# VectorE's order by tile, fixed between the stages of a two-layer encoder

## The chip, the cores and the metric

The kernel runs on one core of one Trainium2 chip. The metric is the device time of one execution in microseconds (us). Before the change three runs took 866.87, 868.81 and 868.93 us, with a median of 868.81 us.

## The reference

The program is an encoder of two layers over 16 learned tokens and 256 input tokens (272 in all) with 1024 channels. In each layer a token mixer and an MLP stand one after the other, and each is wrapped in two norms:

```python
for l in range(DEPTH):                                   # 2 layers
    u = rms_norm(h, norm_mix_pre[l])
    proj = u @ w_in[l]                                   # q, k, v, gates
    y_r = retention_branch(...) @ w_ret_o[l]
    y_a = attention_branch(...) @ w_att_o[l]
    mix = (sigmoid(gate_r) * y_r + sigmoid(gate_a) * y_a) @ w_mix_o[l]
    h = h + rms_norm(mix, norm_mix_post[l])
    u = rms_norm(h, norm_ff_pre[l])
    ff = square(relu(u @ w_ff1[l])) @ w_ff2[l]
    h = h + rms_norm(ff, norm_ff_post[l])
return h[:, N_META:]
```

`rms_norm(x, g)` is `x * rsqrt(mean(x * x) + 1e-6) * g`. `h` is the residual stream. The change touches the two lines that update `h` and the `rms_norm` that reads it at once afterwards.

## The kernel before

**Layout.** Channels lie on the partitions and tokens on the free axis. `h` is eight tiles of 128 channels by 272 tokens (`h[:, k]`, k from 0 to 7). In the second layer's MLP only the last 256 tokens are kept.

**Weights.** 260 units of 128x1024 floats come in turn from memory. `unit` (from L120) reads a unit into `raw`, ScalarE rounds it to `wh` (L131), and VectorE takes the remainder `wl = raw - wh` (L132). The activations are split in the same way. A product of a weight block and an activation tile is three matmuls (L136 to L138): high by high, high weight by low activation (`ul`), low weight by high activation (`uh`). A unit holds eight blocks, one for each `k`, so it is 24 matmuls into one PSUM accumulator. There are four buffers for `wh` and `wl` and three for `raw`.

**Between the stages.** `leave` (L293) drains the products of a stage, scales them into `yg[:, m]` and sums their squares. A mean over the channels is a TensorE product with a constant matrix (L183). Ten matmuls on zeros (L178, `warm(10)`) follow it on TensorE. `rsqrt` makes the factor `y` with Ln and Exp on ScalarE. `leave` hands back `update(k)`. For tile 0 this is four operations of VectorE (L315 and three at L93): `yg` times `y`, a Newton step on it, `h[0]` plus the result, and `y1`, the factor that the other seven tiles use. For each later tile it is two: `yg[k] = -0.5 * yg[k] * y1` and `h[k] = h[k] + yg[k]` (L321).

`enter` (L225) runs `update(k)` for each tile and splits the new `h[k]` times a gain into `uh` (ScalarE, L242) and `ul` (VectorE, through the helper `stt`, so L93). Where the norm asks for it, it also squares `h[k]` (ScalarE, L222) and adds the squares (VectorE, L234, L236). The next stage's products take one tile of `uh` and `ul` at a time. Its first four units are under way at the same time in four accumulators, so a tile feeds twelve matmuls.

**Where this happens.** Three places in the program have a `leave` that is followed by an `enter` with an `update`: the middle of layer 0 (mix to MLP, from 251 us), the border of the layers (MLP of layer 0 to the projections of layer 1, from 447 us) and the middle of layer 1 (from 681 us). They are called the first, second and third place below. The MLP of layer 1 ends in another code.

**What sets the order.** Each engine works through its own list in order. A scheduler makes these lists from the recorded operations when the program is built, by priorities and its own estimates of time. `tc.issue_after(x)` tells it that an operation comes after `x` in its list. At the three places nothing of this kind stands on the operations of `update` and `enter`, so that the scheduler alone decides.

Of the kernel before, what the change touches and what calls it, by code (L numbers as in the profile page):

```python
# [19 lines left out]
KD = D // P  # L20
# [21 lines left out]
def encoder(ctx: ExitStack, tc: tile.TileContext, order, w, h_in, gains, dec, decm, sink, sinkm, tabs, mats, esel, masks, rel, relm, grow, out):  # L42
    nc = tc.nc
    V, A, PE, G = nc.vector, nc.scalar, nc.tensor, nc.gpsimd
    mul, add, sub, mn = ALU.mult, ALU.add, ALU.subtract, ALU.min
# [15 lines left out]
    def slot(i, name, shape=(KD, T), dt=F32):  # L61
        return big.tile([P] + list(shape), dt, tag=f"b{i}", name=name)
# [7 lines left out]
    def tokens(i, name, shape=(KD,), at=32):  # L70
        return slot(i, name, (*shape, ROW), F32R)[..., at:at + T]
# [17 lines left out]
    def f(t):  # L89
        return t.bitcast(F32)  # L90

    def stt(o, a, s, b, op0=mul, op1=mul):
        V.scalar_tensor_tensor(out=o, in0=a, scalar=s, in1=b, op0=op0, op1=op1)  # L93

    def split(xh, xl, x):
        A.activation(xh, x, AF.Copy)  # L96
# [78 lines left out]
    def warm(n):  # L175
        ps = bank("t", [P])
        for _ in range(n):
            tc.keep_in_program_order(PE.matmul(ps, idle, idle, start=True, stop=True))  # L178

    def mean(parts, c0):  # L180
        ms = bank("o", [T])
        for i, p in enumerate(parts):
            PE.matmul(ms[:, c0:], mat["o1024"], p[:, c0:], start=i == 0, stop=i == len(parts) - 1)  # L183
        return ms

    def rsqrt(y1, ms, c0):
        y = two.tile([P, T], F32, tag="t1", name="y")
        w2 = two.tile([P, T], F32, tag="t2", name="w2")
        A.activation(y[:, c0:], ms[:, c0:], AF.Ln)
        A.activation(y[:, c0:], y[:, c0:], AF.Exp, scale=-0.5)  # L190
        return y, w2, newton(None if y1 is None else y1[:, c0:], ms[:, c0:], 0.0, y[:, c0:], w2[:, c0:])

    warm(WARM)
    h = const.tile([P, KD, T], F32, name="h")
    g = const.tile([P, DEPTH, 4, KD], F32, name="g")
# [24 lines left out]
    def square(src, c0):  # L220
        sq = two.tile([P, T], F32, tag="sq", name="sq", bufs=3)
        A.activation(sq[:, c0:], src, AF.Square)  # L222
        return sq

    def enter(l, n, c0, update):  # L225
        x = [tokens(i, "u" + "hl"[i], at=32 - 16 * l) for i in range(2)]
        ss = one.tile([P, T], F32, tag="ss", name="ss")

        lag = KD if n else LAG0

        def accumulate(k):
            sq = square(h[:, k, c0:], c0)
            if k == 0:
                V.tensor_scalar(out=ss[:, c0:], in0=sq[:, c0:], scalar1=8e-6, scalar2=None, op0=add)  # L234
            else:
                V.tensor_tensor(out=ss[:, c0:], in0=ss[:, c0:], in1=sq[:, c0:], op=add)  # L236

        for k in range(KD):
            if update:
                update(k)  # L240
            gk = g[:, l, n, k:k + 1]
            A.activation(x[0][:, k, c0:], h[:, k, c0:], AF.Copy, scale=gk)  # L242
            stt(x[1][:, k, c0:], h[:, k, c0:], gk, f(x[0][:, k, c0:]), op1=sub)
            if k >= lag:
                accumulate(k - lag)
        if update and n == 0:
            for k in range(KD - lag, KD):
                accumulate(k)
        return x, ss, accumulate
# [46 lines left out]
    def leave(l, n, c0, products, init=None):  # L296
        yg = slot(4, "yg")
        ss = one.tile([P, T], F32, tag="ss", name="ss2")
        for m, ps in products:
            sq = square(ps[:, c0:], c0)  # L300
            A.activation(yg[:, m, c0:], ps[:, c0:], AF.Copy, scale=g[:, l, n, m:m + 1])
            if m == 0 and init is None:
                V.tensor_scalar(out=ss[:, c0:], in0=sq[:, c0:], scalar1=8e-6, scalar2=None, op0=add)
            elif m < KD - 1:
                V.tensor_tensor(out=ss[:, c0:], in0=(init if m == 0 else ss)[:, c0:], in1=sq[:, c0:], op=add)
        y1 = one.tile([P, T], F32, tag="rb", name="y1")
        ms = mean([ss, sq], c0)
        warm(10)
        y, w2, sq = rsqrt(None, ms, c0)
        held[len(order) + 3] = [sq.ins]  # L310

        def update(k):
            yk = yg[:, k, c0:]
            if k == 0:
                V.tensor_tensor(out=yk, in0=yk, in1=y[:, c0:], op=mul)  # L315
                stt(yk, w2[:, c0:], 3.0, yk, op0=sub)
                stt(h[:, k, c0:], yk, -0.5, h[:, k, c0:], op1=add)
                stt(y1[:, c0:], w2[:, c0:], 3.0, y[:, c0:], op0=sub)
            else:
                stt(yk, yk, -0.5, y1[:, c0:])  # L320
                V.tensor_tensor(out=h[:, k, c0:], in0=h[:, k, c0:], in1=yk, op=add)  # L321

        return update

# [11 lines left out]
    lows, odds = slice(64, 128), (slice(32, 64), slice(96, 128))  # L336
# [26 lines left out]
    for l in range(DEPTH):  # L363
        c0 = 16 * l
        if l == 0:
            u, ss, early = lead()
        else:
            u, ss, _ = enter(l, 0, 0, update)
            early = [proj(u, 0, "asas"[i], "v_r", i) for i in range(4)]
# [193 lines left out]
        if l == 0:  # L563
# [6 lines left out]
            for c in range(4):  # L570
                V.tensor_tensor(
                    out=pmblk.rearrange("p (t c g k) -> p t c g k", t=4, c=4, g=2)[:, :, c],
                    in0=mat["blk"].rearrange("p (t g k) -> p t g k", t=4, g=2),
                    in1=pm[:, 0:16].unsqueeze(1).unsqueeze(1).to_broadcast([P, 4, 2, 16]),
                    op=mul,
# [187 lines left out]
        def mixed():  # L763
            pair = [product(z, c0, wide(), "mix", m) for m in range(2)]
            for p in pair:
                for _ in range(KD - 1):
                    next(p)
            for m in range(KD):
                *_, (_, ps) = pair[m] if m < 2 else product(z, c0, wide(), "mix", m)
                yield m, ps  # L770

        update = leave(l, 1, c0, mixed())

        u, ss, accumulate = enter(l, 2, c0, update)
        fs, behind = [], []

# [7 lines left out]
        for m in range(KF):  # L784
            if m % KD == 0:
                a, b = ((5, 7), (8, 9), (6, 10), (2, 3))[m // KD]
                low = [tokens(i, "fl", (4,), 32 - c0) for i in ("10a", "10b")] if b == 10 else [tokens(b, "fl", at=32 - c0)]
# [13 lines left out]
        if l == 0:  # L801
            def ff2():
                for m in range(KD):
                    ps = bank(wide(), [T])
                    for q in range(4):
                        wh, wl = unit("ff2", m, q)
                        for k in range(KD):
                            sl = slice(k * P, (k + 1) * P)
                            mm3(ps[:, c0:], wh[:, sl], wl[:, sl], fs[q][0][k][:, c0:], fs[q][1][k][:, c0:], q == 0 and k == 0, q == 3 and k == KD - 1)
                    yield m, ps  # L810

            update = leave(l, 3, c0, ff2(), e2)
# [180 lines left out]
```

## Time and profile before

| | |
|---|---|
| median of three runs | 868.81 us (866.87 to 868.93) |
| the profiled execution | 874.68 us, with a span of 872.9 us |
| TensorE matmuls, busy | 854.7 us (98% of the span) |
| VectorE busy | 608.5 us (70%) |
| ScalarE busy | 564.8 us (65%) |
| mean granted TensorE clock | 0.996 of full |

The span runs from the first to the last instruction of the profiled execution. That execution is 5.87 us longer than the median of the runs without a profile. Busy time of TensorE is that of instructions which overlap, so that 98% does not mean 98% of its peak. The stretches in which TensorE has no matmul are found in the timeline, where a row has in brackets the idle time before it and what ended it.

### The profile page before, as it was taken

How to read it: one execution, taken by the hardware profiler on the slowest of the kernel's cores; microseconds unless marked ns; L12 is line 12 of the kernel's file. 1: busy time of each engine (PE TensorE's matmuls, PEld its weight loads, DVE VectorE, ACT ScalarE, POOL GpSimd, SP SyncE). 2: the span in 40 equal slices, each digit the busy share in tenths (PEclk: the TensorE clock that was granted, in tenths of full speed). 3: DMA queues.
4: the chain of work that ended last, by engine and by line, in shares of the span. 5: the costliest groups of instructions: out<-in, count | busy, mean ns of one | idle time of the engine just before them, and what ended most of it. 6: DMA issues, size and time to landing. Idle time of an engine off the chain costs nothing.

```text
span 872.9 us, 16696 instructions
## 1 busy us (share of the span) xinstructions
PE 854.7 (98%) x6514; PEld 822.2 (94%) x6514; DVE 608.5 (70%) x1129; ACT 564.8 (65%) x1050; POOL 50.6 (6%) x114
## 2 busy tenths in 40 slices
PE   9999999999999999999999999999999999999997
PEld 8899999999989999999989999999999999998885
DVE  7889888878668555444468898888786775554544
ACT  7448788675558777544455578987845587783432
POOL 2112220000000000000000122200000000000000
PEclk9999999999999999999999999999999999999999
DMA  8544443446545655655635544434376276666661
GB/s 293 194 125 139 122 130 114 145 146 192 164 128 179 190 179 178 176 184 172 178 112 153 162 132 141 141 124 148 115 219 200 90 239 189 183 193 194 190 192 70
DMA packets 41407, 142.15 MB, mean 163 GB/s; under 512 B 5360, under 2 KB 6256, under 8 KB 41328
## 3 DMA queue, kind: packets, MB, share of 16 engines
q1 hardware_dynamic: 40896, 140.43, 52.3%
q8 instruction: 51, 0.84, 0.4%
q10 hardware_dynamic: 432, 0.66, 0.2%
q14 instruction: 28, 0.23, 0.1%
HBM read 140.02 MB, written 1.05 MB: 162 GB/s over the span
## 4 chain that ended last, share of the span: by engine, by line
PE 80%; DVE 10%; ACT 6%; issue 1%; DMA 1%; POOL 0%; SPq 0%; DVEq 0%; ACTq 0%; POOLq 0%
PE ps_a L136 12%; PE ps_a L137 12%; PE ps_a L138 12%; PE ps_s L138 5%; PE ps_s L136 5%; PE ps_s L137 5%; PE ps_t L136 4%; PE ps_t L137 4%; PE ps_t L138 4%; DVE wl L132 3%; PE ps_s L853 2%; PE ps_a L853 2%; PE ps_a L855 2%; PE ps_s L855 2%; PE ps_s L854 2%; PE ps_a L854 2%
## 5 line engine op out<-in xcount | busy, mean ns | idle before, releaser
L132 DVE TENSOR_TENSOR wl<-raw,wh 128x1024 fp32r<-128x1024 f32 x256 | 313.0, 1224 | 199.7 <-ACT wh L131 198.2
L131 ACT ACTIVATE wh<-raw 128x1024 fp32r<-128x1024 f32 x256 | 269.8, 1058 | 204.4 <-PE ps_a L137 62.3
L136 PE MATMUL ps_a<-uh,wh 128*128 128x272 f32 (+1 forms) x912 | 263.0, 289 | 2.8 <-ACT uh L242 2.8
L138 PE MATMUL ps_a<-uh,wl 128*128 128x272 f32 (+1 forms) x912 | 260.0, 285 | 0.5 <-DVE wl L132 0.3
L137 PE MATMUL ps_a<-ul,wh 128*128 128x272 f32 (+1 forms) x912 | 260.1, 286 | 0.0
L136 PEld LDWEIGHTS ps_a<-uh,wh 128*128 128x128 f32 x912 | 172.6, 189 | 3.8 <-ACT uh L242 3.2
L138 PEld LDWEIGHTS ps_a<-uh,wl 128*128 128x128 f32 x912 | 172.9, 190 | 1.2 <-DVE wl L132 0.8
L137 PEld LDWEIGHTS ps_a<-ul,wh 128*128 128x128 f32 x912 | 172.4, 189 | 0.4
L138 PE MATMUL ps_s<-uh,wl 128*128 128x272 f32 (+1 forms) x184 | 52.4, 285 | 0.3 <-DVE wl L132 0.3
L137 PE MATMUL ps_s<-ul,wh 128*128 128x272 f32 (+1 forms) x184 | 52.3, 284 | 0.0
L136 PE MATMUL ps_s<-uh,wh 128*128 128x272 f32 (+1 forms) x184 | 52.2, 284 | 0.0
L136 PE MATMUL ps_t<-uh,wh 128*128 128x272 f32 (+1 forms) x152 | 43.5, 286 | 1.3 <-ACT uh L242 1.3
L137 PE MATMUL ps_t<-ul,wh 128*128 128x272 f32 (+1 forms) x152 | 43.5, 286 | 0.0
L138 PE MATMUL ps_t<-uh,wl 128*128 128x272 f32 (+1 forms) x152 | 43.2, 284 | 0.0
L138 PEld LDWEIGHTS ps_s<-uh,wl 128*128 128x128 f32 x184 | 34.9, 190 | 0.5 <-DVE wl L132 0.5
L136 PEld LDWEIGHTS ps_s<-uh,wh 128*128 128x128 f32 x184 | 34.7, 189 | 0.0
L137 PEld LDWEIGHTS ps_s<-ul,wh 128*128 128x128 f32 x184 | 34.6, 188 | 0.0
L136 PEld LDWEIGHTS ps_t<-uh,wh 128*128 128x128 f32 x152 | 28.6, 188 | 1.5 <-ACT uh L242 1.5
L138 PEld LDWEIGHTS ps_t<-uh,wl 128*128 128x128 f32 x152 | 28.9, 190 | 0.0
L137 PEld LDWEIGHTS ps_t<-ul,wh 128*128 128x128 f32 x152 | 28.6, 188 | 0.1
L97 DVE TENSOR_TENSOR fl<-ft,fh 128x272 fp32r<-128x272 f32 (+1 forms) x64 | 27.6, 433 | 1.0 <-ACT fh L96 0.9
L96 ACT ACTIVATE fh<-ft 128x272 fp32r<-128x272 f32 (+1 forms) x64 | 27.2, 425 | 1.7
(311 smaller groups left out, 1963.5 us busy)
## 6 DMA issues: line engine op xcount, KB each, us to landing
raw<-in_w SPq DMA_DIRECT2D x256, 512.0 KB, 3.7
leads<-in_w SPq DMA_DIRECT2D x6, 256.0 KB, 5.6
tab<-in_tabs SPq DMA_DIRECT2D x2, 544.0 KB, 6.3
h<-in_h_in SPq DMA_DIRECT2D x3, 272.0 KB, 5.8
out<-yt SPq DMA_DIRECT2D x3, 256.0 KB, 2.1
leads<-in_w ACTq DMA_DIRECT2D x2, 256.0 KB, 3.4
gj<-in_grow SPq DMA_DIRECT2D x1, 512.0 KB, 4.7
mats<-in_mats SPq DMA_DIRECT2D x1, 320.0 KB, 7.2
```

What stands on the lines that cost most here:

```text
L96: A.activation(xh, x, AF.Copy)
L97: V.tensor_tensor(out=xl, in0=x, in1=f(xh), op=sub)
L131: A.activation(wh[:, c], raw[:, c], AF.Copy)
L132: V.tensor_tensor(out=wl[:, c], in0=raw[:, c], in1=f(wh[:, c]), op=sub)
L136: PE.matmul(ps, ah, bh, start=first, stop=False)
L137: PE.matmul(ps, ah, bl, start=False, stop=False)
L138: return PE.matmul(ps, al, bh, start=False, stop=last)
L853: PE.matmul(pss[i], xh, wh[:, sl], start=kk == 0, stop=False)
L854: PE.matmul(pss[i], xh, wl[:, sl], start=False, stop=False)
L855: PE.matmul(pss[i], xl, wh[:, sl], start=False, stop=kk == KF - 1)
```

## The change

At the three places the operations of VectorE are put in a chain, each told to come after the one before. The chain begins with `h[0]`, then `y1`, and then for each next tile `yg[k]`, `h[k]`, and the low part `ul` of the tile before. The sums of squares, where there are any in this loop, are in the chain too. The first two operations of `update(0)` and the splits of weights (`wl`) are not in it.

```diff
     def stt(o, a, s, b, op0=mul, op1=mul):
-        V.scalar_tensor_tensor(out=o, in0=a, scalar=s, in1=b, op0=op0, op1=op1)
+        return V.scalar_tensor_tensor(out=o, in0=a, scalar=s, in1=b, op0=op0, op1=op1)
...
         lag = KD if n else LAG0
+        line, lows = [], []
+
+        def next_in_line(method, *args, **kw):
+            with ExitStack() as later:
+                if line and update:
+                    later.enter_context(tc.issue_after(line[-1]))
+                line.append(method(*args, **kw).ins)
...
         for k in range(KD):
+            gk = g[:, l, n, k:k + 1]
             if update:
-                update(k)
-            gk = g[:, l, n, k:k + 1]
+                update(k, next_in_line)
             A.activation(x[0][:, k, c0:], h[:, k, c0:], AF.Copy, scale=gk)
-            stt(x[1][:, k, c0:], h[:, k, c0:], gk, f(x[0][:, k, c0:]), op1=sub)
+            low = (x[1][:, k, c0:], h[:, k, c0:], gk, f(x[0][:, k, c0:]))
+            if update:
+                lows.append(low)
+                for low in lows[:-1] if k < KD - 1 else lows:
+                    next_in_line(stt, *low, op1=sub)
+                del lows[:-1]
+            else:
+                stt(*low, op1=sub)
...
-        def update(k):
+        def update(k, put):
             yk = yg[:, k, c0:]
             if k == 0:
                 V.tensor_tensor(out=yk, in0=yk, in1=y[:, c0:], op=mul)
                 stt(yk, w2[:, c0:], 3.0, yk, op0=sub)
-                stt(h[:, k, c0:], yk, -0.5, h[:, k, c0:], op1=add)
-                stt(y1[:, c0:], w2[:, c0:], 3.0, y[:, c0:], op0=sub)
+                put(stt, h[:, k, c0:], yk, -0.5, h[:, k, c0:], op1=add)
+                put(stt, y1[:, c0:], w2[:, c0:], 3.0, y[:, c0:], op0=sub)
             else:
-                stt(yk, yk, -0.5, y1[:, c0:])
-                V.tensor_tensor(out=h[:, k, c0:], in0=h[:, k, c0:], in1=yk, op=add)
+                put(stt, yk, yk, -0.5, y1[:, c0:])
+                put(V.tensor_tensor, out=h[:, k, c0:], in0=h[:, k, c0:], in1=yk, op=add)
```

The lists of the engines change at the three places and nowhere else; those of GpSimd and SyncE stay as they were. In the lists below, a name ends in the number of its buffer, and "x2" is two equal rows.

VectorE at the first place, before. `w2_3383` is the Newton step's factor, `y1_3367` the factor of tiles 1 to 7, `uh_3388` and `ul_3389` the high and low part of the new stream:

```order
L93 SCALAR_TENSOR_TENSOR yg_3086<-w2_3383,yg_3086 128x272
L93 SCALAR_TENSOR_TENSOR y1_3367<-w2_3383,y_3382 128x272
L93 SCALAR_TENSOR_TENSOR h_90<-yg_3086,h_90 128x272
L93 SCALAR_TENSOR_TENSOR yg_3086<-yg_3086,y1_3367 128x272 x2
L93 SCALAR_TENSOR_TENSOR ul_3389<-h_90,g_91,uh_3388 128x272
L321 TENSOR_TENSOR h_90<-h_90,yg_3086 128x272 x2
```

Later in the same list, still before the change, `wl_3523` stands between the last `yg` and the last `h`. It is the low part of the fourth unit that the MLP's first products use:

```order
L93 SCALAR_TENSOR_TENSOR ul_3389<-h_90,g_91,uh_3388 128x272 x2
L321 TENSOR_TENSOR h_90<-h_90,yg_3086 128x272
L93 SCALAR_TENSOR_TENSOR yg_3086<-yg_3086,y1_3367 128x272
L132 TENSOR_TENSOR wl_3523<-raw_3520,wh_3522 128x1024
L93 SCALAR_TENSOR_TENSOR ul_3389<-h_90,g_91,uh_3388 128x272
L321 TENSOR_TENSOR h_90<-h_90,yg_3086 128x272
```

VectorE at the first place, with the change:

```order
L93 SCALAR_TENSOR_TENSOR yg_3086<-w2_3383,yg_3086 128x272
L132 TENSOR_TENSOR wl_3523<-raw_3520,wh_3522 128x1024
L93 SCALAR_TENSOR_TENSOR h_90<-yg_3086,h_90 128x272
L93 SCALAR_TENSOR_TENSOR y1_3367<-w2_3383,y_3382 128x272
L93 SCALAR_TENSOR_TENSOR yg_3086<-yg_3086,y1_3367 128x272
L236 TENSOR_TENSOR h_90<-h_90,yg_3086 128x272
L93 SCALAR_TENSOR_TENSOR ul_3389<-h_90,g_91,uh_3388 128x272
```

The split of the fourth weight unit has moved from near the end of the tiles to a place ahead of `h[0]`, `h[0]` has changed places with `y1`, and the first `ul` now stands behind `yg[1]` and `h[1]`. From there the list goes on in threes: `yg`, `h`, `ul`. At the second place the list begins in the same way, with the split of that stage's fourth unit ahead of `h[0]`.

VectorE at the third place, before, where sixteen more operations stand between the last row and the fourth unit's split (`wl_9016`):

```order
L93 SCALAR_TENSOR_TENSOR yg_8579<-w2_8876,yg_8579 128x256
L93 SCALAR_TENSOR_TENSOR y1_8860<-w2_8876,y_8875 128x256
L93 SCALAR_TENSOR_TENSOR h_90<-yg_8579,h_90 128x256
L93 SCALAR_TENSOR_TENSOR yg_8579<-yg_8579,y1_8860 128x256 x2
L93 SCALAR_TENSOR_TENSOR ul_8882<-h_90,g_91,uh_8881 128x256
```

VectorE at the third place, with the change:

```order
L93 SCALAR_TENSOR_TENSOR yg_8579<-w2_8876,yg_8579 128x256
L93 SCALAR_TENSOR_TENSOR h_90<-yg_8579,h_90 128x256
L93 SCALAR_TENSOR_TENSOR y1_8860<-w2_8876,y_8875 128x256
L132 TENSOR_TENSOR wl_9016<-raw_9013,wh_9015 128x1024
L93 SCALAR_TENSOR_TENSOR yg_8579<-yg_8579,y1_8860 128x256
L236 TENSOR_TENSOR h_90<-h_90,yg_8579 128x256
L93 SCALAR_TENSOR_TENSOR ul_8882<-h_90,g_91,uh_8881 128x256
```

Here `h[0]` comes first, and the split stands between `y1` and everything of tile 1.

TensorE at the first place, before, from the fourth matmul of tile 0 (L136 takes `uh` and `wh`, L137 `ul` and `wh`, L138 `uh` and `wl`):

```order
L136 MATMUL ps_a_3526<-uh_3388,wh_3522 128x272
L137 MATMUL ps_a_3433<-ul_3389,wh_3429 128x272
L138 MATMUL ps_a_3433<-uh_3388,wl_3430 128x272
L137 MATMUL ps_t_3464<-ul_3389,wh_3460 128x272
L138 MATMUL ps_t_3464<-uh_3388,wl_3461 128x272
L137 MATMUL ps_s_3495<-ul_3389,wh_3491 128x272
L138 MATMUL ps_s_3495<-uh_3388,wl_3492 128x272
L137 MATMUL ps_a_3526<-ul_3389,wh_3522 128x272
L136 MATMUL ps_a_3433<-uh_3388,wh_3429 128x272
```

TensorE at the first place, with the change, from the same matmul:

```order
L136 MATMUL ps_a_3526<-uh_3388,wh_3522 128x272
L137 MATMUL ps_a_3433<-ul_3389,wh_3429 128x272
L138 MATMUL ps_a_3433<-uh_3388,wl_3430 128x272
L136 MATMUL ps_a_3433<-uh_3388,wh_3429 128x272
L137 MATMUL ps_t_3464<-ul_3389,wh_3460 128x272
L138 MATMUL ps_t_3464<-uh_3388,wl_3461 128x272
L136 MATMUL ps_t_3464<-uh_3388,wh_3460 128x272
L137 MATMUL ps_s_3495<-ul_3389,wh_3491 128x272
L138 MATMUL ps_s_3495<-uh_3388,wl_3492 128x272
L136 MATMUL ps_s_3495<-uh_3388,wh_3491 128x272
```

In both lists the four matmuls on `uh[0]` come first and the fifth takes `ul[0]`. With the change the matmuls on `uh[1]` stand in between those on `ul[0]`, and most of the fourth accumulator's matmuls (`ps_a_3526`) come later.

## Rows read from the trace of the kernel before

**Rows 1.** The page, part 1: busy us of each engine (share of the span) xinstructions.

```profile
PE 854.7 (98%) x6514; PEld 822.2 (94%) x6514; DVE 608.5 (70%) x1129; ACT 564.8 (65%) x1050; POOL 50.6 (6%) x114
```

**Rows 2.** Waits: engine, line, awaited; total us, times, longest us.

```profile
PE ps_a L136 <- ACT uh L242: 2.8, 2, 1.4
...
PE ps_t L136 <- ACT uh L242: 1.3, 1, 1.3
```

**Rows 3.** Timeline of VectorE, first place: start, duration, instruction, [idle before].

```profile
254.08 0.44 DVE L167 TENSOR_TENSOR w<-ps_o,w 128x272 f32<-128x272 f32 x1
254.55 0.44 DVE L93 SCALAR_TENSOR_TENSOR yg<-w,yg 128x272 f32<-128x272 f32 x1
254.91 0.43 DVE L93 SCALAR_TENSOR_TENSOR y<-w,y 128x272 f32<-128x272 f32 x1
255.26 0.43 DVE L93 SCALAR_TENSOR_TENSOR h<-yg,h 128x272 f32<-128x272 f32 x1
...
256.32 0.49 DVE L93 SCALAR_TENSOR_TENSOR ul<-h,g,uh 128x272 fp32r<-128x272 f32 x1
256.73 0.79 DVE L321 TENSOR_TENSOR h<-h,yg 128x272 f32<-128x272 f32 x2
...
262.67 1.22 DVE L132 TENSOR_TENSOR wl<-raw,wh 128x1024 fp32r<-128x1024 f32 x1
263.81 0.49 DVE L93 SCALAR_TENSOR_TENSOR ul<-h,g,uh 128x272 fp32r<-128x272 f32 x1
```

**Rows 4.** Timeline of ScalarE, first place.

```profile
253.95 1.04 ACT L131 ACTIVATE wh<-raw 128x1024 fp32r<-128x1024 f32 x1
255.73 0.52 ACT L242 ACTIVATE uh<-h,g 128x272 fp32r<-128x272 f32 x1 [0.74 <-DVE h L93]
```

**Rows 5.** Timeline of TensorE, first place.

```profile
249.79 0.29 PE L136 MATMUL ps_t<-zh,wh 128*128 128x272 f32 x1
249.92 0.29 PE L137 MATMUL ps_t<-zl,wh 128*128 128x272 f32 x1
...
256.31 0.39 PE L136 MATMUL ps_a<-uh,wh 128*128 128x272 f32 x1 [1.39 <-ACT uh L242]
...
256.91 0.36 PE L137 MATMUL ps_a<-ul,wh 128*128 128x272 f32 x1
```

**Rows 6.** Timeline of TensorE, second place.

```profile
451.82 0.39 PE L136 MATMUL ps_a<-uh,wh 128*128 128x272 f32 x1 [1.39 <-ACT uh L242]
...
461.49 0.39 PE L138 MATMUL ps_s<-uh,wl 128*128 128x272 f32 x1 [0.29 <-DVE wl L132]
...
465.15 0.72 PE L183 MATMUL ps_o<-ss,mats 128*128 128x272 f32 x2
```

**Rows 7.** Timeline of VectorE, third place.

```profile
684.50 0.42 DVE L93 SCALAR_TENSOR_TENSOR h<-yg,h 128x256 f32<-128x256 f32 x1
684.84 0.76 DVE L93 SCALAR_TENSOR_TENSOR yg<-yg,y 128x256 f32<-128x256 f32 x2
```

**Rows 8.** Timeline of TensorE, third place.

```profile
685.51 0.38 PE L136 MATMUL ps_t<-uh,wh 128*128 128x256 f32 x1 [1.27 <-ACT uh L242]
...
686.09 0.33 PE L137 MATMUL ps_t<-ul,wh 128*128 128x256 f32 x1
```

**Rows 9.** Stretches, layer 0 and first place: busy us by engine, PEclk, DMA share, GB/s.

```profile
40.10:43.10 3.00, 1.14 (x8) 0.94 (x8) 2.81 (x6) 0.87 (x3) 1.81 (x3) 1.00 0.65 184
43.10:46.50 3.40, 3.40 (x17) 3.40 (x16) 1.26 (x4) 1.06 (x1) 0.00 (x0) 0.50 0.42 148
...
254.90:256.30 1.40, 0.02 (x1) 0.00 (x0) 1.40 (x5) 0.66 (x3) 0.00 (x0) 1.00 0.00 0
```

**Rows 10.** Timeline of TensorE in layer 0, at the lower and the full clock.

```profile
42.68 0.49 PE L434 MATMUL ps_s<-mats,pads 128*128 128x128 f32 x2 [0.98 <-POOL pads L429]
...
43.59 0.43 PE L136 MATMUL ps_a<-uh,wh 128*128 128x272 f32 x1
43.82 0.43 PE L137 MATMUL ps_a<-ul,wh 128*128 128x272 f32 x1
```

More of the change, by code (lines that the diff above doesn't have):

```diff
@@ L233, in accumulate @@
             if k == 0:
-                V.tensor_scalar(out=ss[:, c0:], in0=sq[:, c0:], scalar1=8e-6, scalar2=None, op0=add)
+                next_in_line(V.tensor_scalar, out=ss[:, c0:], in0=sq[:, c0:], scalar1=8e-6, scalar2=None, op0=add)
             else:
-                V.tensor_tensor(out=ss[:, c0:], in0=ss[:, c0:], in1=sq[:, c0:], op=add)
+                next_in_line(V.tensor_tensor, out=ss[:, c0:], in0=ss[:, c0:], in1=sq[:, c0:], op=add)
         for k in range(KD):
+            gk = g[:, l, n, k:k + 1]
             if update:
-                update(k)
-            gk = g[:, l, n, k:k + 1]
+                update(k, next_in_line)
             A.activation(x[0][:, k, c0:], h[:, k, c0:], AF.Copy, scale=gk)
-            stt(x[1][:, k, c0:], h[:, k, c0:], gk, f(x[0][:, k, c0:]), op1=sub)
+            low = (x[1][:, k, c0:], h[:, k, c0:], gk, f(x[0][:, k, c0:]))
[6 more added lines that the diff above has]
+                stt(*low, op1=sub)
             if k >= lag:
```

## The prediction

> **What bounds the kernel now.** I read the page first. TensorE's matmuls are busy for 98% of the span, VectorE for 70% [rows 1], so time is lost or won where TensorE stands still, and the list of waits says where that is. Between the stages it waits three times for the first `uh` of the new stream, for 1.4, 1.4 and 1.3 us [rows 2]. The timelines of the three places show why. The reader should follow one chain there: VectorE's factor, `h[0]`, ScalarE's `uh[0]`, TensorE's first matmul. At the first place `h[0]` starts at 255.26 [rows 3], `uh[0]` at 255.73 [rows 4], the first matmul at 256.31 [rows 5]. From then on TensorE has a matmul about every 0.125 us (249.79 to 249.92 is such a step [rows 5]), and a tile feeds twelve of them, 1.5 us. So the start of the stream counts in full, and behind it only a first `ul` or a second `uh` that is too late.
>
> **The prices on VectorE.** An operation that needs nothing of the one before it starts 0.35 us after it (254.91 to 255.26), one that needs its result 0.47 us after it (254.08 to 254.55), and behind a `ul` the step is 0.41 us (256.32 to 256.73) [rows 3]. The split of a weight unit holds the list for 1.14 us (262.67 to 263.81) [rows 3].
>
> **First place.** The change puts the split of the fourth unit ahead of `h[0]`. The split needs `wh`, which ScalarE ends at 253.95 + 1.04 = 254.99 [rows 4]; with the hand-over of 0.07 us that lies between the end of `uh` (256.25) [rows 4] and the start of `ul` (256.32) [rows 3], it starts at 255.06. `h[0]` follows at 255.06 + 1.14 = 256.20 in place of 255.26, and the first matmul comes 0.94 us later, at 257.25. Everything in the chain is queued behind the split; ScalarE waits with `uh[0]`, and TensorE for that.
>
> Then `ul[0]`. It now stands behind `y1`, `yg[1]` and `h[1]`, of which the last two each need the operation in front of them: 256.20 + 0.35 + 0.47 + 0.47 + 0.35 = 257.84, against 256.32 before. It runs 0.49 us, and with a hand-over of 0.07 us TensorE has it at 258.40; before, it took `ul[0]` at 256.91 [rows 5]. By then it has done the four matmuls on `uh[0]` and stood still since about 257.85, so 0.55 us are lost anew. From there a tile costs VectorE 0.47 + 0.35 + 0.41 = 1.23 us, and TensorE's list wants nine or ten matmuls for it, 1.13 to 1.25 us: about even, and the fourth accumulator's matmuls that were put off fill the end. Against it stand small stops that the old order had after its start, and which I estimate at 0.25 us from the steps of more than 0.125 us in its timeline. So 0.94 + 0.55 - 0.25, about 1.2 us. The bounds are 0.9 (only the start counts) and 1.5 (nothing comes back).
>
> **Second place.** The list begins alike, so 0.94 + 0.55 us are lost in the same way, from a first matmul at 451.82 [rows 6]. What comes back is larger. TensorE waited for the split of the fourth unit at 461.49, with 0.29 us idle [rows 6]; that split is now early. But the sum of squares ends on the same list, and the norm of layer 1 waits for it (the mean at 465.15 [rows 6]). VectorE's list is longer by seven steps of 0.47 in place of 0.35 us, 0.8 us, and some of what its waits add. If the norm decides, 1.3 us are lost; if TensorE's row of matmuls does, 0.6. With the split done early, its `raw` buffer is free some 8 us sooner, and the next transfers start sooner. No row prices that; it can take back at most a few tenths of the waits after the norm. I take 1.1 us, from 0.3 to 1.4.
>
> **Third place.** `h[0]` goes ahead of `y1` and gains one step, 0.34 us (684.50 to 684.84 is such a step [rows 7]). But the split now stands between `y1` and tile 1. From `h[0]` at 684.16: `y1` 684.50, the split 684.84, `yg[1]` 685.98, `h[1]` 686.43, `ul[0]` 686.77. TensorE, which got `ul[0]` at 686.09 [rows 8], gets it at about 687.32. It starts at 685.2 in place of 685.51 [rows 8], does four matmuls and stands still for 1.5 us. Net 1.23 us, less small stops as above: 1.0 us, from -0.3 (the earlier start is kept and other matmuls fill the gap) to 1.3.
>
> One rule of the Trainium skill speaks against the longer steps. VectorE: DVE Perf Modes, section "The DRAIN you can't avoid", says that after every operation the next starts only when the pipe has emptied, so that leaving out the semaphore between two of them gains nothing. By that rule the new order by tile would cost VectorE no more than the old, and the sum would be smaller by the two dependent steps ahead of the first `ul`, some 0.7 us over the three places. The trace differs: 0.35 us without a dependence, 0.47 with one [rows 3].
>
> **The clock.** TensorE's clock can fall. In layer 0 it was idle for 0.98 us before a row of two small matmuls [rows 10], in a stretch of 3.0 us in which it was busy for 1.14 us; after that the granted clock was 0.50, the lower level of 1.2 GHz, from 43.10 to 46.50 [rows 9], and the matmuls came every 0.23 us (43.59 to 43.82 [rows 10]) in place of 0.125. Some 15 of them ran so, which cost 15 x 0.10 = 1.5 us. At the first place the idle 1.4 us of before, behind the ten warming matmuls, kept the clock at 1.00 [rows 9]. With the change that idle time is 1.39 + 0.94 = 2.3 us at the first two places, and after four matmuls TensorE stands still again for 0.6 us: less work than in the stretch that lost the clock. At the third place it is 1.1 and 1.5 us. Where the fall comes exactly differs from run to run, I suppose, so I count one fall in the typical run, at 1.3 us, since part of the slow time lies in a wait.
>
> **The sum.** 1.2 + 1.1 + 1.0 = 3.3 us of waiting, and 1.3 us for the clock: 4.6 us. Against the profiled execution's own time that is 874.68 + 4.6 = 879.3 us. The median of the runs shown is 5.87 us below the profiled execution, so 868.81 + 4.6 = 873.4 us. Elsewhere the lists are the same, but for a few places at which sums of squares of layer 0 move among the MLP's first units; TensorE has 24 matmuls, 3 us, for each of those, which hide an add of 0.44 us.
>
> **The rivals.**
> - *The clock holds.* The waits are as above, but no fall follows: 868.81 + 3.3 = 872.1 us. For it: 1.4 us of idle time did not lower the clock [rows 9]. Against it: less idle time in one piece did, in rows 9 and 10. The Trainium skill (TensorE: Matmul & The Clock Gate, section "HAM oscillation — how this bites in real kernels") has the clock fall after idle gaps longer than any that I foresee here, and by that rule this rival is the case. The fall at 43.10 shows that shorter ones can do it.
> - *It falls more often.* Two or three falls, at 1.5 us: 868.81 + 3.3 + 3.8 = 875.9 us.
> - *The delay is given back.* Were the lost time in the first two stages only that of the start, and the earlier transfers and the split that is out of the way saved the rest, 0.9 + 0.3 + 0 = 1.2 us would remain: 870.0 us. The rows against it are those of `ul[0]`.
> - *Faster.* The stream runs without a stop from an earlier start. It needs the split not to hold `h[0]`, so that `h[0]` comes one step earlier at each of the three places (3 x 0.35 = 1.05 us), and the tiles in threes to take away every later stop, which I estimate at 0.6, 1.5 and 0.6 us from the matmul starts of the three places: 868.81 - 3.75 = 865.1 us. It decides at one point, whether VectorE does the split before or after `h[0]` and `ul[0]`. The lists put it before.
> - *The change doesn't do what it says.* The order by tile does stand in the lists, so I give this nothing of its own.
>
> **How the numbers follow.** The forecast of 873.4 us gets 0.34, with a range of its own from 872.5 to 874.5; the clock that holds 0.27; more falls 0.17; given back 0.18; faster 0.04. A change under 0.3%, 2.6 us, can't be told from none by such a measurement. So slower begins at 871.4 us: 0.34 + 0.17 and 0.20 of the 0.27, 0.71. Faster ends at 866.2: 0.04. The rest is 0.25. The range runs from 870.6 to 876.6 us: it leaves out the faster case, half of the case that is given back, and the top of the case with more falls.
>
> **What would show it.** In the profile after, at the first two places: a `wl` of 1.2 us right ahead of VectorE's `h[0]`, the wait of TensorE for `uh[0]` at 2.3 us in place of 1.4, and a second wait of 0.5 to 0.6 us for the first `ul`. At the third: a wait for `uh[0]` some 0.3 us shorter, and one of about 1.5 us for `ul`. In the threes, 0.47 us from `yg` to `h`. A granted clock of 0.5 for a few us right behind one of the places, or at none of them, tells the forecast from the first two rivals. The prediction is wrong if the fifth matmul at each place follows the fourth without a stop, or if the border's norm comes no later than its first matmul does.

## The result, and the profile after

The changed kernel takes 875.26 us, the median of five runs (872.94 to 877.13), and the kernel before 868.71 us (866.87 to 868.93). The ratio is 1.0077, with a 95% interval from 1.0056 to 1.0099: slower by 6.6 us, where 4.6 us were forecast.

The changed kernel's profiled execution took 875.75 us, with a span of 874.0 us, only 1.1 us more than the profiled execution of before. That small difference misleads; the last part explains it. What answers to [rows 1] is the first part of the page, busy us of each engine:

```profile
PE 852.1 (97%) x6514; PEld 819.5 (94%) x6514; DVE 610.2 (70%) x1129; ACT 565.4 (65%) x1050; POOL 51.6 (6%) x114
```

The same instructions are there and nearly the same busy time. So the shares of busy time say nothing, and the waits have to be read. Of TensorE in the changed kernel (line, awaited, total us, times, longest us), beside [rows 2]:

```profile
PE ps_a L136 <- ACT uh L249: 4.6, 2, 2.3
PE ps_t L137 <- DVE ul L93: 1.4, 1, 1.4
PE ps_t L136 <- ACT uh L249: 1.1, 1, 1.1
PE ps_a L137 <- DVE ul L93: 0.8, 2, 0.4
```

Before there were 4.1 us in three waits; now it is 7.9 us in six. The two rows with `ul` are new: TensorE starts the stream and stands still again. VectorE's timeline at the first place shows both reasons, beside [rows 3]:

```profile
251.84 1.23 DVE L132 TENSOR_TENSOR wl<-raw,wh 128x1024 fp32r<-128x1024 f32 x1
252.98 0.43 DVE L93 SCALAR_TENSOR_TENSOR h<-yg,h 128x272 f32<-128x272 f32 x1
253.33 0.43 DVE L93 SCALAR_TENSOR_TENSOR y<-w,y 128x272 f32<-128x272 f32 x1
253.80 0.44 DVE L93 SCALAR_TENSOR_TENSOR yg<-yg,y 128x272 f32<-128x272 f32 x1
254.28 0.44 DVE L236 TENSOR_TENSOR h<-h,yg 128x272 f32<-128x272 f32 x1
254.64 0.49 DVE L93 SCALAR_TENSOR_TENSOR ul<-h,g,uh 128x272 fp32r<-128x272 f32 x1
```

The reader should subtract the starts. The split `wl` stands ahead of `h[0]` and holds it for 1.14 us (251.84 to 252.98). Then come four steps of 0.35, 0.47, 0.48 and 0.36 us until `ul[0]` starts, 1.66 us behind `h[0]`; before, it was 1.06 us. TensorE at the same place, beside [rows 5]:

```profile
254.02 0.39 PE L136 MATMUL ps_a<-uh,wh 128*128 128x272 f32 x1 [2.29 <-ACT uh L249]
...
254.50 0.28 PE L136 MATMUL ps_a<-uh,wh 128*128 128x272 f32 x1
255.19 0.39 PE L137 MATMUL ps_a<-ul,wh 128*128 128x272 f32 x1 [0.41 <-DVE ul L93]
...
255.69 0.43 PE L137 MATMUL ps_t<-ul,wh 128*128 128x272 f32 x1
255.92 0.43 PE L138 MATMUL ps_t<-uh,wl 128*128 128x272 f32 x1
```

It waits for 2.29 us in place of 1.39, does four matmuls, waits for 0.41 us, and then its matmuls come 0.23 us apart in place of 0.125: the clock has fallen. At the third place `h[0]` is early, but the split stands between the factor and tile 1, as VectorE shows, beside [rows 7]:

```profile
686.82 0.42 DVE L93 SCALAR_TENSOR_TENSOR y<-w,y 128x256 f32<-128x256 f32 x1
687.16 1.22 DVE L132 TENSOR_TENSOR wl<-raw,wh 128x1024 fp32r<-128x1024 f32 x1
...
689.08 0.48 DVE L93 SCALAR_TENSOR_TENSOR ul<-h,g,uh 128x256 fp32r<-128x256 f32 x1
```

and TensorE, beside [rows 8]:

```profile
687.50 0.39 PE L136 MATMUL ps_t<-uh,wh 128*128 128x256 f32 x1 [1.05 <-ACT uh L249]
...
689.62 0.58 PE L137 MATMUL ps_t<-ul,wh 128*128 128x256 f32 x1 [1.38 <-DVE ul L93]
```

The clock is read from stretches (length; busy us of PE, PEld, DVE, ACT and POOL with their instructions; granted clock; DMA share; GB/s). Of the changed kernel, beside [rows 9]:

```profile
255.60:259.00 3.40, 3.40 (x17) 3.40 (x17) 3.33 (x9) 1.88 (x4) 0.00 (x0) 0.50 0.12 48
453.60:457.00 3.40, 3.40 (x17) 3.40 (x17) 3.30 (x10) 1.89 (x5) 0.00 (x0) 0.50 0.13 52
689.10:692.50 3.40, 2.88 (x13) 2.89 (x14) 3.30 (x10) 1.53 (x3) 0.00 (x0) 0.50 0.47 154
43.10:46.50 3.40, 3.40 (x30) 3.40 (x29) 2.13 (x5) 1.06 (x1) 0.00 (x0) 1.00 0.47 147
```

It fell to 0.50 behind each of the three places, for 3.4 us each, and not at 43 us, where it fell before.

**Where the time is.** The stages can be measured from the matmul that begins each norm's mean. In the kernel before (layer 1's norm, at 465.15, is in [rows 6]):

```profile
251.31 0.39 PE L183 MATMUL ps_o<-ss,mats 128*128 128x272 f32 x1
307.24 0.39 PE L183 MATMUL ps_o<-ss,mats 128*128 128x272 f32 x1
446.82 0.39 PE L183 MATMUL ps_o<-ss,mats 128*128 128x272 f32 x1
...
680.68 0.45 PE L183 MATMUL ps_o<-ss,mats 128*128 128x256 f32 x1
```

and in the changed kernel:

```profile
248.13 0.39 PE L183 MATMUL ps_o<-ss,mats 128*128 128x272 f32 x1
306.69 0.39 PE L183 MATMUL ps_o<-ss,mats 128*128 128x272 f32 x1
446.27 0.39 PE L183 MATMUL ps_o<-ss,mats 128*128 128x272 f32 x1
467.39 0.50 PE L183 MATMUL ps_o<-ss,mats 128*128 128x272 f32 x1
682.88 0.45 PE L183 MATMUL ps_o<-ss,mats 128*128 128x256 f32 x1
```

The stage that begins with the first place lasted 55.93 us and now lasts 58.56; the stretch from the border of the layers to layer 1's norm lasted 18.33 and now lasts 21.12; the stretch between them is 139.58 us in both, and the one from layer 1's norm to the third place 215.53 and 215.49 us. The last place, from 680.68 or 682.88 to the end of the span, is compared at one and the same step of the dense matmuls (see the last part): 191.09 us after, and 189.07 us in the execution of the kernel before that had that step there too, which is the one timed against itself below. That is 2.6 + 2.8 + 2.0 = 7.4 us, and it all lies at the three places. Ahead of the first place the changed kernel's execution was shorter, for reasons that the last part gives.

### The profile page after: what moved, and what is told of

Its sections match the earlier page's. It is cut to its first block, busy times and chain, and to the rows that moved or that the text cites. A ratio compares the mean times of both kernels' runs of the same rounds, so it can differ in the third digit from the quotient of the medians.

```text
span 874.0 us, 16695 instructions
## 1 busy us (share of the span) xinstructions
PE 852.1 (97%) x6514; PEld 819.5 (94%) x6514; DVE 610.2 (70%) x1129; ACT 565.4 (65%) x1050; POOL 51.6 (6%) x114
## 4 chain that ended last, share of the span: by engine, by line
PE 80%; DVE 10%; ACT 6%; issue 2%; DMA 1%; POOL 0%; SPq 0%; DVEq 0%; ACTq 0%; POOLq 0%
PE ps_a L137 12%; PE ps_a L138 12%; PE ps_a L136 12%; PE ps_s L137 5%; PE ps_s L138 5%; PE ps_s L136 5%; PE ps_t L137 4%; PE ps_t L136 4%; PE ps_t L138 4%; DVE wl L132 4%; PE ps_a L868 2%; PE ps_s L868 2%; PE ps_s L867 2%; PE ps_a L867 2%; PE ps_s L869 2%
## 5 line engine op out<-in xcount | busy, mean ns | idle before, releaser
L136 PE MATMUL ps_a<-uh,wh 128*128 128x272 f32 (+1 forms) x912 | 262.4, 288 | 4.6 <-ACT uh L249 4.6
L137 PE MATMUL ps_a<-ul,wh 128*128 128x272 f32 (+1 forms) x912 | 259.3, 285 | 0.8 <-DVE ul L93 0.8
L138 PE MATMUL ps_a<-uh,wl 128*128 128x272 f32 (+1 forms) x912 | 259.7, 285 | 0.3 <-DVE wl L132 0.3
L136 PEld LDWEIGHTS ps_a<-uh,wh 128*128 128x128 f32 x912 | 172.7, 189 | 5.7 <-ACT uh L249 5.0
L137 PEld LDWEIGHTS ps_a<-ul,wh 128*128 128x128 f32 x912 | 172.6, 189 | 1.3 <-DVE ul L93 1.2
L138 PEld LDWEIGHTS ps_a<-uh,wl 128*128 128x128 f32 x912 | 172.4, 189 | 0.8 <-DVE wl L132 0.7
L137 PE MATMUL ps_s<-ul,wh 128*128 128x272 f32 (+1 forms) x184 | 52.9, 288 | 0.0
L136 PE MATMUL ps_s<-uh,wh 128*128 128x272 f32 (+1 forms) x184 | 52.6, 286 | 0.0
L138 PE MATMUL ps_s<-uh,wl 128*128 128x272 f32 (+1 forms) x184 | 52.6, 286 | 0.0
L137 PE MATMUL ps_t<-ul,wh 128*128 128x272 f32 (+1 forms) x152 | 43.5, 286 | 1.4 <-DVE ul L93 1.4
L136 PE MATMUL ps_t<-uh,wh 128*128 128x272 f32 (+1 forms) x152 | 43.4, 286 | 1.1 <-ACT uh L249 1.1
L138 PE MATMUL ps_t<-uh,wl 128*128 128x272 f32 (+1 forms) x152 | 43.4, 285 | 0.0
L137 PEld LDWEIGHTS ps_s<-ul,wh 128*128 128x128 f32 x184 | 35.7, 194 | 0.0
L136 PEld LDWEIGHTS ps_s<-uh,wh 128*128 128x128 f32 x184 | 35.4, 193 | 0.0
L138 PEld LDWEIGHTS ps_s<-uh,wl 128*128 128x128 f32 x184 | 35.3, 192 | 0.0
L137 PEld LDWEIGHTS ps_t<-ul,wh 128*128 128x128 f32 x152 | 29.0, 191 | 1.6 <-DVE ul L93 1.6
L136 PEld LDWEIGHTS ps_t<-uh,wh 128*128 128x128 f32 x152 | 29.2, 192 | 1.2 <-ACT uh L249 1.2
L138 PEld LDWEIGHTS ps_t<-uh,wl 128*128 128x128 f32 x152 | 29.2, 192 | 0.0
L795 ACT ACTIVATE ft<-ft 128x272 f32<-128x272 f32 (+1 forms) x64 | 27.2, 425 | 1.6
```

The costliest lines, as they stand in the source:

```text
L136: PE.matmul(ps, ah, bh, start=first, stop=False)
L137: PE.matmul(ps, ah, bl, start=False, stop=False)
L138: return PE.matmul(ps, al, bh, start=False, stop=last)
L795: A.activation(t2[:, c0:], t1[:, c0:], AF.Square)
```

## The experiments

Theory A: the loss is that the split stands ahead of `h[0]`, that `ul[0]` comes late, and that TensorE's clock falls behind these stops. The rivals: the order in threes itself (`yg`, `h`, `ul` of one tile behind each other, each waiting for the last) costs the time, or the clock is beside the point. For each kernel the table gives how much longer than in the kernel before its three stretches were, from the starts of the same matmuls in its profile, and the timed ratio.

| kernel | first | border | third | sum, us | ratio (95%) | mean clock |
|---|---|---|---|---|---|---|
| changed | 2.6 | 2.8 | 2.0 | 7.4 | 1.0077 (1.0056 to 1.0099) | 0.9928 |
| changed, again | 2.6 | 2.8 | 2.5 | 7.9 | 1.0084 (1.0064 to 1.0105) | 0.9928 |
| 20 idle matmuls | 1.4 | 1.5 | 1.4 | 4.3 | 1.0059 (1.0033 to 1.0085) | 0.9976 |
| `ul[0]` put back | 1.1 | 2.6 | 0.8 | 4.5 | 1.0060 (1.0038 to 1.0082) | 0.9946 |
| split put back | 0.7 | 2.4 | 0.6 | 3.7 | 1.0050 (1.0028 to 1.0073) | 0.9955 |
| split back, 20 idle | 0.9 | 1.4 | 1.1 | 3.4 | 1.0041 (1.0020 to 1.0062) | 0.9968 |
| both put back | 0.6 | 1.3 | 0.6 | 2.5 | 1.0036 (1.0017 to 1.0054) | 0.9976 |
| both back, again | 0.6 | 1.3 | 0.6 | 2.5 | 1.0024 (1.0002 to 1.0045) | 0.9978 |
| both, split behind `yg[4]` | 0.6 | 1.3 | 0.7 | 2.5 | 1.0034 (1.0015 to 1.0053) | 0.9976 |
| spread order | 0.4 | 0.8 | 0.6 | 1.8 | 1.0007 (0.9990 to 1.0025) | 0.9979 |
| spread order, again | 0.4 | 0.8 | 0.5 | 1.7 | 1.0006 (0.9990 to 1.0023) | 0.9977 |
| kernel before, 3 idle | | 0.4 | 0.1 | | 1.0030 (1.0009 to 1.0051) | 0.9913 |
| kernel before | 0 | 0 | 0 | 0 | 0.9992 (0.9972 to 1.0012) | 0.9977 |

The last column is the mean granted clock over the runs of that kernel; 88 runs of the kernel before beside them gave 0.9977. One fall of 3.4 us to a half, in 872 us, is 0.0020, so the column counts falls beyond those of before: 2.5 in a run of the changed kernel. It is a rough count, since every profile here shows one more fall at its end, of which 1.3 to 4.5 us lie in the span. The stretches are those of one profile of each kernel.

**The split put behind `ul[1]`.**

```diff
                 A.activation(wh[:, c], raw[:, c], AF.Copy)
+                for ins in held_low.get(i, ()):
+                    later.enter_context(tc.issue_after(ins))
                 V.tensor_tensor(out=wl[:, c], in0=raw[:, c], in1=f(wh[:, c]), op=sub)
...
+        if update:
+            held_low[len(order) + 3] = [line[7]]
```

> The changed kernel, with the split of the fourth weight unit told to come after ul[1] at each of the three places; the chain stays as it is. Theory A (the split ahead of h[0] and of tile 1 is what costs, by the wait itself and by the clock that falls after it): first matmul 0.2 to 0.35 us sooner than in the kernel before at each place, a wait of 0.5 us for ul[0], no fall of the granted clock at the places, and a time of 868.5 to 870.5 us against 868.7 before. Theory B (the order in threes, with its dependent steps of 0.47 us, is what costs): most of the loss stays, 873 to 876 us.

Measured: 874.70 us against 869.68, ratio 1.0050. The wait for the first `uh` went down as it should, even under that of before, but a stop for `ul[0]` is there at every place:

```profile
PE ps_a L139 <- ACT uh L252: 2.3, 2, 1.2
PE ps_t L139 <- ACT uh L252: 1.1, 1, 1.1
PE ps_a L140 <- DVE ul L93: 0.8, 2, 0.4
PE ps_t L140 <- DVE ul L93: 0.4, 1, 0.4
```

The clock still fell at the border, in the profile once and by the mean 1.1 times a run more than before. The expectation of A was missed, and the time lies in B's range. But in the stretches the loss went from 7.4 to 3.7 us: the split is a part of it, and only a part.

**20 idle matmuls in place of 10 behind the mean**, in the changed kernel:

```diff
-        warm(10)
+        warm(20)
```

> The changed kernel with twenty warming matmuls on zeros in place of ten, which run while TensorE waits for uh[0]; VectorE's list stays as it is. Theory A (waits of some 3.3 us and clock falls of 1.0 to 1.5 us each, up to three): the waits of VectorE's chain stay, the granted clock stays at 1.00 at the three places, and the time is 871.5 to 872.8 us. Theory B (the clock alone is the loss): 868.5 to 869.5 us. Theory C (the clock costs nothing, since TensorE then waits for VectorE anyway): 875 us as with ten.

Measured: 874.67 us, ratio 1.0059. The clock held at all three places, in the stretches of that kernel's profile:

```profile
255.60:259.00 3.40, 2.99 (x22) 2.78 (x23) 3.30 (x9) 2.14 (x6) 0.00 (x0) 1.00 0.52 154
452.40:455.80 3.40, 2.95 (x21) 2.63 (x21) 3.30 (x9) 2.14 (x7) 0.00 (x0) 1.00 0.47 154
687.50:690.90 3.40, 2.93 (x26) 2.73 (x25) 3.30 (x9) 1.28 (x3) 0.00 (x0) 1.00 0.47 154
```

At the first two places nothing else changed: the first matmul comes 5.9 us behind the mean's, as in the changed kernel. At the third the idle matmuls themselves hold the first matmul by 0.9 us, but `ul[0]`, for which TensorE then waits 0.5 us in place of 1.4, comes no later. So the waits alone cost 4.3 us, and the three falls the rest of 7.4: 1.2, 1.3 and 0.7 us. The timed loss, 5.1 us, lies above A's range and nearer to the expectation that the clock matters little; its interval does not part it from the changed kernel's. The stretches and the mean clock part them.

**The kernel before with 3 idle matmuls**, to lower the clock without touching VectorE's order:

```diff
-        warm(10)
+        warm(3)
```

> The kernel before, with three warming matmuls on zeros in place of ten at the three places; VectorE's list is that of the kernel before. TensorE is idle for about 3.0 us in place of 1.4 there, and everything else waits for nothing new. Theory A: the granted clock falls to 0.5 behind each place in most runs, and each fall costs 1.0 to 1.5 us, so 871.5 to 873.5 us. Theory C (the clock costs nothing or does not fall by idle time of this length): 868.7 us.

Measured: 872.17 us, ratio 1.0030, 2.6 us. TensorE's idle time before the first matmul grew to twice that of before, with the work as late as ever:

```profile
PE ps_a L136 <- ACT uh L242: 5.9, 2, 3.0
PE ps_t L136 <- ACT uh L242: 2.8, 1, 2.8
```

The mean clock is 0.9913, 3.3 falls more than before, so a fall costs 0.8 us here: less than 1.5, since at the border, for instance, the late matmuls catch up and 0.4 us remain. The clock alone slows this kernel. A is right there, though not at every place: in the profile the clock fell behind 2.95 us of idle time at the first two places, and held at 1.00 behind 2.83 us at the third. The first stretch has no entry, because part of it ran at the other step of the dense matmuls.

**A spread order.** `h[0]` first, the split behind `yg[4]`, and at tiles 1, 3 and 4 a `ul` between `yg` and the `h` that needs it:

```diff
+TURN = "h0 y1 yg1 ul0 h1 yg2 h2 ul1 yg3 ul2 h3 yg4 ul3 h4 yg5 h5 ul4 yg6 h6 ul5 yg7 h7 ul6 ul7"
...
+            for at, what in enumerate(TURN.split()):
...
+                next_in_line(method, *args, **kw)
+                if at == HOLD:
+                    held_low[len(order) + 3] = [line[-1]]
```

> A chain in another order at the three places: h[0], y1, yg[1], ul[0], h[1], yg[2], h[2], ul[1] and so on, with the split of the fourth unit after yg[4]. Theory A: first matmul 0.25 to 0.35 us sooner than in the kernel before, ul[0] without a wait of over 0.1 us, no clock fall, small waits of 0.2 to 0.3 us later; 867.8 to 869.2 us, about the kernel before. Theory B (any fixed order by tile costs): 871 us or more.

Measured: 870.14 us against 869.68, ratio 1.0007: as the kernel before, and not faster. That is A as a difference; 870.14 us itself lies above its range. The first matmul comes 0.23 us earlier (4.77 us behind the mean's, in place of 5.00), and small stops behind it give back more than that: at the first place the stream's first 96 matmuls took 13.12 us in place of 12.45. No clock fell at the places.

**`ul[0]` ahead of `h[1]`, the split left in front.**

```diff
                 line.append(method(*args, **kw).ins)
+            if len(line) == 3 and lows:
+                next_in_line(stt, *lows.pop(0), op1=sub)
```

> The changed kernel with one step put back: ul[0] stands ahead of h[1] (order wl, h0, y1, yg1, ul0, h1, then threes); the 1.14 us split is still ahead of h[0]. A (waits, and the clock falls only where the second stop for ul[0] follows the first): at the first two places the wait for uh[0] stays at 2.3 us, that for ul[0] (0.4 us) is gone, the third place keeps about 1.1 us for ul[0]; clock holds at the first two: kernel before plus 2.5 to 4 us, ratio 1.003 to 1.0045. B (the 2.3 us stop alone lowers the clock): falls at the first two places as in the changed kernel, kernel before plus 5 to 6.5 us, ratio 1.006 to 1.0075. C (the threes behind are the cost): no change against the changed kernel, with the clock held.

Measured: 875.51 us against 869.49, ratio 1.0060, B by its number. The waits are those expected: 2.3 us for `uh[0]` twice, nothing for `ul[0]` at these places, and 0.9 us at the third.

```profile
PE ps_a L136 <- ACT uh L251: 4.6, 2, 2.3
PE ps_t L136 <- ACT uh L251: 1.1, 1, 1.1
PE ps_t L137 <- DVE ul L93: 0.9, 1, 0.9
```

The clock held at the first place and fell at the border, and the mean is 1.6 falls below before's. So one stop of 2.3 us is enough in some runs and not in others; the second stop is not needed, though there were more falls with it.

**The split put back, with 20 idle matmuls.**

> The changed kernel with the split behind ul[1], and 20 idle matmuls instead of 10 after the mean. A (what was left of the loss with the split moved was the clock and a 0.4 to 0.5 us wait for ul[0] at each place): clock at 1.00 at all three places, first matmul 0.2 us earlier than in the kernel before, stages 0.6 to 0.7 us longer: kernel before plus 1.5 to 2.5 us, ratio 1.0015 to 1.003. B (the order in threes costs in another way that the stages do not show): 1.005 or more, as without the 20.

Measured: 872.83 us, ratio 1.0041, above A's range and below B's. The clock held at the three places, but here the remedy is a cost of its own, as TensorE's timeline shows:

```profile
251.21 4.63 PE L181 MATMUL ps_t<-idle 128*128 128x128 f32 x40
255.59 0.37 PE L139 MATMUL ps_a<-uh,wh 128*128 128x272 f32 x1
```

Each of the 20 idle matmuls is two rows there. They last until the stream's first matmul, with no gap: it comes 5.59 us behind the mean, and 4.77 us with 10 of them, in the kernel that differs in nothing else. What keeps the clock up must fit into the wait that it fills.

**Both put back, the threes kept** (the two diffs above together):

> The changed kernel with both steps put back: the split behind ul[1], ul[0] ahead of h[1]; the threes yg, h, ul behind them stay. A (those two steps are the loss): waits for uh[0] 1.2 us as before, none over 0.3 us behind it, clock held, stages 0.3 to 0.5 us longer than in the kernel before: ratio 1.000 to 1.002. B (the threes themselves cost 4 to 5 us): 1.005 or more.

Measured: 874.05 us, ratio 1.0036. Only the waits for the first `uh` are left, and each is shorter than before:

```profile
PE ps_a L139 <- ACT uh L254: 2.3, 2, 1.2
PE ps_t L139 <- ACT uh L254: 1.1, 1, 1.1
```

Yet the stretches are 2.5 us longer. The ratio lies above A's range, and only the lower end of its interval within it; for B it is too small. To settle this and the noise, three kernels were timed again beside one new one.

**The kernel before against itself.**

> The kernel before against itself, to see what the comparison makes of no change at all. Both theories: ratio 0.998 to 1.002. If it falls outside, differences of 1 to 3 us between two kernels of this study mean nothing.

Measured: 0.9992 (0.9972 to 1.0012). A difference of 1 us means nothing here, one of 2 to 3 us something.

**Both put back, again.**

> The kernel with both steps put back and the threes kept, once more beside the one whose order spreads the dependent steps. A (the threes cost by themselves): 2 us or more over that one, ratio 1.003 to 1.0045 against the kernel before. B (the first time was the draw of the matmul step's level): ratio 1.000 to 1.002, within 1 us of that one.

Measured: 873.81 us, ratio 1.0024 (1.0002 to 1.0045), between A and B.

**Both put back, with the split behind `yg[4]`** (`line[11]` in place of `line[7]`).

> Both steps put back, threes kept, and the split another step later, behind yg[4] instead of yg[3], as in the kernel with the spread order. A (the split's place is what parts these two): as the spread order, ratio 0.9995 to 1.0015. B (the threes): as the kernel with both steps put back.

Measured: 873.49 us, ratio 1.0034, stretches equal to those with the split behind `yg[3]`: B. The split's place there doesn't matter.

**The spread order, again.**

> The spread order once more (h0 y1 yg1 ul0 h1 yg2 h2 ul1 yg3 ul2 h3 yg4, then the split). A: ratio 0.999 to 1.002 as the first time. B (the first time was the draw of the matmul step's level): 1.002 to 1.004.

Measured: 871.82 us against 870.14, ratio 1.0006. So A, by the ratio.

**The changed kernel, again**, beside the kernels with steps put back:

> The changed kernel once more, beside the others of this call. Both theories: ratio 1.006 to 1.009; waits of 2.3 us for uh[0] at the first two places and 1.4 us for ul[0] at the third. A (the clock falls behind these stops, but not in each execution): a fall of 3.4 us at two or three of the three places; C (the three falls of the first profile were chance): none or one.

Measured: 877.25 us against 869.49, ratio 1.0084. The waits are the same to 0.1 us, and the clock fell at all three places again.

What follows: of the 7.4 us in the stretches about 5 go with the two steps, the split ahead of `h[0]` or tile 1 and `ul[0]` behind `h[1]`, and with the falls of the clock behind them. With both put back 2.5 us are left, 0.7 more than with the spread order (1.8), most of it at the border (1.3 against 0.8). The ratios say 1.5 to 2.5 us between these two, with intervals that overlap.

At the border the traces show one more thing. The last sums of squares, for which layer 1's mean waits, stand on VectorE behind the split of a later unit. Before, one sum stands behind it:

```profile
463.52 1.23 DVE L132 TENSOR_TENSOR wl<-raw,wh 128x1024 fp32r<-128x1024 f32 x1 [0.29 <-ACT wh L131]
464.66 0.43 DVE L236 TENSOR_TENSOR ss<-ss,sq 128x272 f32<-128x272 f32 x1
```

With the chain there are two, here with both steps put back, and the mean behind them on TensorE:

```profile
461.88 1.23 DVE L135 TENSOR_TENSOR wl<-raw,wh 128x1024 fp32r<-128x1024 f32 x1 [0.28 <-ACT wh L132]
463.02 0.98 DVE L239 TENSOR_TENSOR ss<-ss,sq 128x272 f32<-128x272 f32 x2
464.15 0.41 PE L186 MATMUL ps_o<-ss,mats 128*128 128x272 f32 x1
```

From the start of that split to the mean it is 1.63 us before (the mean is at 465.15) and 2.27 here; it is 2.18 in the changed kernel and in the spread order. So 0.5 to 0.6 us of what every order with the chain loses at the border lie behind that split. VectorE is idle for 0.3 us ahead of it in both kernels, so the length of its list up to there is not what decides. TensorE's list moves too: the mean stands behind 96 matmuls of the new stream before, behind 101 in the changed kernel, 104 in the spread order and 105 with both steps put back. No run moved these sums or the mean alone, so what the threes cost by themselves at the border is not shown.

Why the spread order's stretches lose 1.8 us where its time loses only 0.5 us stays open too; 1.8 us is a ratio of 1.0021, within both of its intervals. No order tried here is faster than that of the kernel before.

## Why the prediction came out as it did

**The mechanism was right**, except for the end of the border's stretch. The places, the waits and their causes are those foretold: `wl` ahead of `h[0]`, 2.3 us for `uh[0]` (2.29 measured), the first matmul 0.94 us later by forecast and 0.90 measured (5.9 behind the mean's in place of 5.0), a second wait of 0.5 to 0.6 us (0.4 shown as idle, 0.55 beyond a usual step), and at the third place a wait 0.2 us shorter and one of 1.4 us for `ul[0]` (forecast 0.3 and 1.5). The steps of 0.35 and 0.47 us came out as read.

**The sum of the waits was too small**: 3.3 us by forecast, 4.3 measured with the clock held, 1.4, 1.5 and 1.4 us in place of 1.2, 1.1 and 1.0. The term that failed is the credit for small stops, "which I estimate at 0.25 us", at the first and third place. Nothing of it came back: at the first place the stream's first 96 matmuls took 12.45 us before and 12.99 with the clock held, 0.54 us more, which is the stop for `ul[0]` alone. Without the credit the forecast's own terms give 0.94 + 0.55 = 1.5 and 1.23 us. At the border 1.5 us lie just above the upper bound of 1.4, and not for the reason given. The forecast had the norm wait for a list of VectorE that grew by longer steps. With the clock held, the split that stands ahead of the last sums started 0.93 us later than before, and VectorE was idle for 0.27 us ahead of it, so its list was not full. The other 0.55 us are those of the second sum that now stands behind that split, a term that the forecast did not have. The wait of 0.29 us for the fourth unit's split did go, without bringing the loss below that.

**The clock was counted too low.** One fall at 1.3 us was forecast; there are about 2.5 a run more than before, and in both profiles three of three places have one. Their price was right in size: 1.2, 1.3 and 0.7 us. The failed step is "I count one fall in the typical run". It rested on one fall in layer 0 in one profile; that place falls in some runs and not in others in the kernel before too, so a profile with one fall told that such stops can lower the clock, and not how often three of them would. Of the rivals, the one with two or three falls, 875.9 us, comes nearest to 875.26, with waits too small and a price of a fall too high: that its sum comes so near is luck.

**The other rivals.** The clock doesn't hold: the rule in the Trainium skill (TensorE: Matmul & The Clock Gate, section "HAM oscillation — how this bites in real kernels") would have kept it at 1.00, and stops of 2.3 and 0.4 us, and of 1.1 and 1.4 us, lowered it in both profiles of the changed kernel. Nothing was given back: the stretch of 139.58 us behind the first stage is equal to 0.01 us in both, and earlier transfers of the weights show nowhere. Faster needed the split behind `ul[0]`; with it there, the best kernel only equals the one before.

**The steps on VectorE.** VectorE: DVE Perf Modes in the Trainium skill, section "The DRAIN you can't avoid", has it that a semaphore between two operations costs nothing extra. The trace differs here too: 0.35 us to `y1`, which needs nothing of `h[0]`, and 0.47 us from `y1` to `yg[1]`, which needs it, in the changed kernel. The same section also says that a next operation which is not held starts earlier, which the prediction left out. The trace agrees: the 0.35 us are less than the 0.43 us that the operation in front takes. What the longer steps cost in all is not shown. Of the orders fixed by hand, the one that parts some of the dependent operations is the only one whose border stretch loses less than 1 us, but what stands behind the last split there is the same in all of them, and no run parted the two.

**Range and chances.** 875.26 us lies in the range, and slower was the likeliest sign. The forecast's own narrow range, 872.5 to 874.5 us, missed it by 0.8 us.

## What to carry to other kernels

When an order is fixed by hand, look at what is left free: here the chain pinned the stream's operations behind each other, and the one long operation outside the chain, a split of 1.14 us, slid in front of them. Look as well at what else moved in the lists: at the border a second sum came to stand behind another such split. Price the stops and what TensorE's clock makes of them separately, and count how often the clock falls from the mean granted clock of many runs, not from one profile. Compare stage by stage between the same two instructions, since the whole span of one execution can differ by 8 us for reasons that are not the kernel's: the spread order's two profiled executions spanned 868.9 and 877.0 us.

## What was not expected of the hardware

Dense matmuls had two steps in these profiles (a step is the time from one start to the next), and a stage mostly kept the one that it had. The same program, the kernel before, in two executions; 40 us of steady matmuls in layer 0 and in layer 1. In the profile of the kernel before:

```profile
200.00:240.00 40.00, 40.00 (x318) 40.00 (x317) 29.28 (x45) 19.75 (x29) 0.00 (x0) 1.00 0.63 194
700.00:740.00 40.00, 40.00 (x342) 40.00 (x342) 25.41 (x33) 32.45 (x64) 0.00 (x0) 1.00 0.69 213
```

and in the profile of the same kernel timed against itself:

```profile
200.00:240.00 40.00, 40.00 (x326) 40.00 (x325) 29.45 (x46) 20.64 (x31) 0.00 (x0) 1.00 0.69 205
700.00:740.00 40.00, 40.00 (x355) 40.00 (x355) 25.25 (x32) 33.16 (x63) 0.00 (x0) 1.00 0.69 212
```

The granted clock is 1.00 in all four, and TensorE is never idle, but 318 matmuls are done in one and 326 in the other, 342 and 355 in layer 1. From the starts in the trace the step is 123.33 or 126.66 ns at 272 columns, 113.33 or 117.78 ns at 256. The profiles here had now the one, now the other, stage by stage. The span moves without a change of the program: 872.9 us in the first of these two executions, 865.4 us in the second. Of the difference 2.5 us lie ahead of the first place, some of them for the fall at 43 us, which the second does not have, 1.8 us between layer 1's norm and the third place, and 3.2 us behind it. This is why the spans of before and after differ by 1.1 us and the medians by 6.6: the profiled execution of before had the longer step ahead of the first place and behind the third, that of after the shorter; the stretch ahead of the first place was 3.2 us shorter for it and for the fall at 43 us that did not come, and the one behind the third would have been 3.2 us longer at the other step. What sets the step was not found.
